# A two-layer hybrid block on one core: the root taken of the tanh, the input gate multiplied from PSUM, weight high parts on ScalarE in one stretch, key tiles read from PSUM

## The chip, the core and the metric

The kernel runs on one core of a Trainium2 chip. The metric is the device time of one execution in microseconds; lower is better. The kernel before took 1835.72 us as the median of 3 runs (1835.39 to 1839.09).

## The reference

Two layers act on 256 latent and 256 context tokens of width 1024. A layer normalises and modulates, runs four branches side by side (a state-space branch, grouped-query attention, differential attention and a gated linear recurrence), merges them with sigmoid gates, and ends in a convolutional feed-forward part. The last layer gives out the latent tokens alone. The change touches the recurrence and the keys of the grouped-query attention:

```python
def rglru_sequence(x_in, p, h0):                       # recurrence, 512 channels, both directions
    xr = dwconv(x_in, p['rg_conv_w'], p['rg_conv_b'], 1)
    for d in range(2):
        gate_a = blockdiag(xr, p['rg_wa'][d]) + p['rg_ba'][d]
        gate_x = blockdiag(xr, p['rg_wx'][d]) + p['rg_bx'][d]
        log_a = -8 * sigmoid(gate_a) * softplus(-p['rg_lambda'][d])
        a = exp(log_a)
        b = sqrt(-expm1(2 * log_a)) * (sigmoid(gate_x) * xr)
        h_sum += linear_scan(a, b, h0[d])              # context first, then latent
    return h_sum                                       # then times gelu(rgg)

kc = rmsnorm(heads(k_c), p['gqa_knorm_g'])             # keys of the context
kl = apply_rope(rmsnorm(heads(k_l), p['gqa_knorm_g']), cos, sin)
```

## The kernel before

Every matmul operand in fp32 is split into a high part, rounded to the fast matmul type, and a low part, the rest; a product is three matmuls (`mm3`, L267 to L269: low by high, high by low, high by high). `split` makes the parts: the high one by a cast, on ScalarE (L256, ACT in the profile) or on VectorE (L258, DVE), the low one by a subtraction (L251) on GpSimd (POOL) or DVE. For weights `whl` (L319) does so in tiles of 128x1024 named `whl`, four buffers of them. `turn` sets the engines by counting tiles: `turn[1]` is how often a low part goes to POOL, `turn[2]` how often a high part goes to DVE. In the stretch from the first recurrent pair to the end of the state-space branch `turn[1:] = 1, 2` holds: every low part on POOL, every second high part on DVE.

PSUM is two pools of four buffers each: `big` for projections, `small` for the rest. A `big` tile is free again when its last reader is done. The order of instructions on each engine is not written out: a scheduler with a timeline of its own chooses it when the program is built, so that a change in one function can move instructions elsewhere. On each engine instructions run in that order, and one that waits holds up those behind it.

In each layer, after the norm, the recurrent inputs are projected (`rg_in`), then come `rg_pair(0)`, `kvdt`, `rg_pair(1)`, `xbc(0)` and the state-space branch, beside which the recurrent branch is merged (`merge(3, ...)`).

`rg_pair` works on two channel tiles `c` by two directions `d`. Two small matmuls (L1021, L1024) give the gates; ACT takes tanh of both (L1022 to `t` in tile `B`, L1025 to `tx`), then exp (L1027, to `e`) and tanh (L1028, in `t`) of the decay. With `t` = tanh(u/2) and `e` = exp(-u), DVE forms 1 - a (L1030), minus (1 - a squared) (L1031) and a (L1032) on 128x1024; one ACT instruction takes the root for all of the pair (L1033, 128x2048, behind a load of its function table). DVE multiplies the gate (L1038), POOL the input (L1040, four of 128x512), then DVE scans (L1041, L1042, L1044), POOL adds the directions (L1054), DVE multiplies by the gelu (L1055) and the result is split into `bo` (ACT L256, DVE L251). The gelu of the second projection `rgg` stands between (L1048 to L1052).

`kvdt` (L652) projects key, step size and value columns for four token tiles into `big`, copies keys and steps to SBUF as `raw` (ACT L666, in a buffer called `xs`) and values (DVE L667), then works on all four together: squares (L671), sums (L673), the power on POOL (L676), rotary products (L608 to L619), scaling (L682), transposes on PE (L625) and the split into `kp`. `ssd_decay` follows with the softplus of the step sizes (L343 to L356).

Of the kernel before, what the change touches and what calls it, by code (L numbers as in the profile page):

```python
# [9 lines left out]
F32 = mybir.dt.float32  # L10
# [8 lines left out]
T = NL + NX  # L19
# [188 lines left out]
def _build(ctx, nc, tc, I, out, dbg):  # L208
# [19 lines left out]
    def big(n=T):  # L228
        p = pb.tile([128, 512], F32, name="big")
        return p[:, :n]  # L230
# [5 lines left out]
    def tt(name, n=512, dt=F32, bufs=None):  # L236

        x = tmp.tile([128, 512], dt, name=name, bufs=bufs or 3)
        return x[:, :n]
# [4 lines left out]
    def blk(ap, d):  # L244
        return ap.rearrange("p (h d) -> p h d", d=d)

    def bc(ap, shape):
        return ap.to_broadcast(shape)
# [287 lines left out]
    def tm(ps, w, t, h):  # L536

        kn = w[0].h.shape[1]
        for k in range(KT):
            mm3(ps, h[:, k, t * 128:(t + 1) * 128], w[k // kn][:, k % kn], k == 0, k == KT - 1)  # L540
# [14 lines left out]
    class Mixer:  # L555
# [96 lines left out]
        def kvdt(self):  # L652

            l, p, h = self.l, self.p, self.h
            w = wrows(l, "kvdt0", 2) + wrows(l, "kvdt1", 2)
            kp = self.long([128, 2, 2, T], "kp", 1, F32R)
            kh, kl = kp[:, 0], kp[:, 1]
            self.gk = Mat(kh, kl)
            self.gv = self.long([128, 4, 128], "gv")
            self.dt = sp.tile([128, 4, 16], F32, name="dt", bufs=1)  # L660
            raw = self.long([128, 2, T], "xs", 2).rearrange("p a t -> p (a t)")[:, :576]
            raw = raw.rearrange("p (t c) -> p t c", t=4)
            for t in range(4):
                ps = big(272)
                tm(ps, w, t, h)
                S.copy(raw[:, t], ps[:, 0:144])  # L666
                V.tensor_copy(self.gv[:, t], ps[:, 144:272])  # L667
            V.tensor_tensor(self.dt, raw[:, :, 128:144], bc(p["dtb"][:, None, :], [128, 4, 16]), op=OP.add)
            k = raw[:, :, 0:128]
            sq = tt("sq", bufs=2)  # L670
            S.activation(blk(sq, 128), k, AF.Square)  # L671
            ss = sp.tile([128, 8], F32, name="ss")
            V.tensor_reduce(ss, blk(sq, 64), axis=AX.X, op=OP.add)  # L673
            V.tensor_scalar(ss, ss, 1.0 / 64, EPS, op0=OP.mult, op1=OP.add)
            r = sp.tile([128, 8], F32, name="r64")
            G.tensor_tensor(r, ss, mhalf[:, :8], op=OP.pow)  # L676
            for t in range(0, 4, 2):
                d = blk(tt("fo", 256), 64)
                for z in range(2):
                    self.rope_of(d[:, 2 * z:2 * z + 2], blk(k[:, t + z], 64), t + z, 1, 2)  # L680
                d2 = tt("fo")
                V.tensor_tensor(d2.rearrange("p (h z c) -> p h z c", h=4, z=2), bc(d[:, :, None, :], [128, 4, 2, 64]),  # L682
                                bc(r[:, 2 * t:2 * t + 4, None, None], [128, 4, 2, 64]), op=OP.mult)
                v = self.twice(d2)
                for z in range(2):
                    ts = slice((t + z) * 128, (t + z + 1) * 128)
                    self.keys(v[:, 2 * z:2 * z + 2], kh[:, :, ts], kl[:, :, ts])
# [320 lines left out]
        def rg_pair(self, i, bm, xrs, bws):  # L1008

            l, p, h, n = self.l, self.p, self.h, self.n  # L1010

            es = [self.long([128, 2, T], "st", 3) for _ in range(2)]
            ta = self.long([128, 4, T], "B8")
            ts = [ta[:, 2 * c:2 * c + 2] for c in range(2)]
            xs = [self.long([128, 2, T], "st", 3), self.long([128, 2, T], "A4")]
            for c in range(2):
                for d in range(2):
                    pc = d * 4 + 2 * i + c
                    t, e, tx = ts[c][:, d], es[c][:, d], xs[c][:, d]
                    ps = small()  # L1020
                    PE.matmul(ps, bws[c][:, d * 2], xrs[c], start=True, stop=True)  # L1021
                    S.activation(t, ps, AF.Tanh, scale=0.5, bias=p["rba"][:, pc:pc + 1])  # L1022
                    px = small()
                    PE.matmul(px, bws[c][:, d * 2 + 1], xrs[c], start=True, stop=True)  # L1024
                    S.activation(tx, px, AF.Tanh, scale=0.5, bias=p["rbx"][:, pc:pc + 1])  # L1025
                    c1, c2 = p["rgc"][:, pc:pc + 1], p["rgm"][:, pc:pc + 1]
                    S.activation(e, t, AF.Exp, scale=c2, bias=c2)  # L1027
                    S.activation(t, t, AF.Tanh, scale=c1, bias=c1)  # L1028
                e2 = es[c]
                V.scalar_tensor_tensor(e2, e2, 1.0, ts[c], op0=OP.add, op1=OP.mult)  # L1030
                V.scalar_tensor_tensor(ts[c], e2, -2.0, e2, op0=OP.add, op1=OP.mult)  # L1031
                V.tensor_scalar(e2, e2, -1.0, 1.0, op0=OP.mult, op1=OP.add)  # L1032
            S.activation(ta, ta, AF.Sqrt, scale=-0.25)  # L1033
            wg = wcols(l, f"rgg{i}")
            for c in range(2):
                cp = 2 * i + c
                t, e, tx = ts[c], es[c], xs[c]
                V.scalar_tensor_tensor(tx, tx, 1.0, t, op0=OP.add, op1=OP.mult)  # L1038
                for d in range(2):
                    G.tensor_tensor(tx[:, d], tx[:, d], xrs[c], op=OP.mult)  # L1040
                V.tensor_tensor_scan(t[:, 0, NL:T], e[:, 0, NL:T], tx[:, 0, NL:T], 0.0, op0=OP.mult, op1=OP.add)  # L1041
                V.tensor_tensor_scan(t[:, 0, 0:NL], e[:, 0, 0:NL], tx[:, 0, 0:NL], t[:, 0, T - 1:T], op0=OP.mult,  # L1042
                                     op1=OP.add)
                V.tensor_tensor_scan(t[:, 1, ::-1], e[:, 1, ::-1], tx[:, 1, ::-1], 0.0, op0=OP.mult, op1=OP.add)  # L1044
                ps = big(n)
                fm(ps, wg[c], h, n)
                u = tt("sq", n, bufs=2)
                S.activation(u, ps, AF.Square)  # L1048
                V.tensor_scalar(u, u, 0.044715, 1.0, op0=OP.mult, op1=OP.add)
                V.tensor_tensor(u, u, ps, op=OP.mult)  # L1050
                S.activation(u, u, AF.Tanh, scale=math.sqrt(2.0 / math.pi))
                V.scalar_tensor_tensor(u, u, 1.0, ps, op0=OP.add, op1=OP.mult)  # L1052
                f = t[:, 0, :n]
                G.tensor_tensor(f, f, t[:, 1, :n], op=OP.add)  # L1054
                V.scalar_tensor_tensor(f, f, 0.5, u, op0=OP.mult, op1=OP.mult)  # L1055
                split(bm[cp][:, :n], f, V)
# [178 lines left out]
    for l in range(DEPTH):  # L1235
# [14 lines left out]
        turn[1] = NEVER  # L1250
        b3 = mx.branch()
        rin = [mx.rg_in(0, "bcm", 1), mx.rg_in(1, "xs", 2)]
        turn[1:] = 1, 2
        mx.rg_pair(0, b3, *rin[0])
        late_params(l, p)
        mx.kvdt()
# [92 lines left out]
```

## Time and profile before

| what | value |
|---|---|
| median of the runs | 1835.72 us |
| profiled execution, its own time | 1833.32 us |
| its span | 1831.2 us |
| mean granted clock of TensorE, share of full speed | 0.963 |
| PE busy | 1715.3 us, 94% |
| DVE busy | 1298.7 us, 71% |
| ACT busy | 904.4 us, 49% |
| POOL busy | 889.1 us, 49% |

The span is what the profile shows of an execution; its own time has 2.1 us around that. PE is TensorE's matmuls, whose ends are modelled, so its share says how much of the span had a matmul under way. Layer 0's recurrence and keys lie at about 70 to 190 us of the span, layer 1's at about 1170 to 1290 us. Durations of neighbours on one engine overlap by up to a tenth of a us.

### The profile page before, as it was taken

Reading aid. Unit: us, or ns where it says so; the run is one execution under the profiler, and the core shown is the slowest. Engines: PE = TensorE matmul, PEld = TensorE weight load, DVE = VectorE, ACT = ScalarE, POOL = GpSimd, SP = SyncE. Lnnn points to the kernel's source line nnn. Section 1 sums busy time; section 2 is a strip of 40 time slices with the busy share of each in tenths; the row PEclk is TensorE's granted clock in tenths of the full one; section 3 lists DMA queues with packets and bytes.
Section 4 is the critical chain, followed back from the end, with each engine's and each line's share of the span. In section 5 each row is a group of like instructions: output and inputs, shape, how many; then the busy total and the mean of one; then the engine's idle time right before and its main releaser. Section 6 shows DMA issues by size and latency. Waiting matters only on the chain.

```text
span 1831.2 us, 27922 instructions
## 1 busy us (share of the span) xinstructions
PE 1715.3 (94%) x10734; PEld 1499.3 (82%) x10734; DVE 1298.7 (71%) x2259; ACT 904.4 (49%) x1651; POOL 889.1 (49%) x536
## 2 busy tenths in 40 slices
PE   7968999999989998999999999966989999989999
PEld 1856788878788787987888888855888899989998
DVE  6798667666868676898856475698867668567664
ACT  3525544545444554465544343535445455556554
POOL 4364656252435657566543242465574244534443
PEclk8988999999989999999999999978989999989999
DMA  7211433131313355535645443222233133445553
GB/s 290 85 69 46 145 104 122 70 104 47 104 58 111 112 184 207 185 119 172 219 172 181 147 147 111 69 83 97 93 117 137 47 116 113 164 141 196 181 182 130
DMA packets 52036, 237.10 MB, mean 129 GB/s; under 512 B 9664, under 2 KB 12608, under 8 KB 34496
## 3 DMA queue, kind: packets, MB, share of 16 engines
q1 hardware_dynamic: 28080, 179.46, 28.1%
q10 hardware_dynamic: 23824, 55.86, 9.6%
q8 instruction: 85, 1.39, 0.3%
q14 instruction: 47, 0.39, 0.1%
HBM read 234.18 MB, written 1.11 MB: 128 GB/s over the span
## 4 chain that ended last, share of the span: by engine, by line
PE 44%; DVE 9%; DMA 2%; POOL 2%; ACT 2%; issue 2%; DVEq 0%; ACTq 0%; POOLq 0%; SPq 0%
PE big L267 13%; PE big L268 13%; PE big L269 13%; DVE whl L251 1%; DMA w<-in_w 1%; DVE fo L435 1%; POOL whl L251 1%; DVE fo L552 1%; DMA wa<-in_w 1%; PE small L781 1%; PE small L589 1%; ACT whl L256 1%; DVE whl L258 0%; DVE B L1044 0%; PE small L1021 0%
## 5 line engine op out<-in xcount | busy, mean ns | idle before, releaser
L251 POOL TENSOR_TENSOR whl<-w,whl 128x1024 fp32r<-128x1024 f32 (+3 forms) x194 | 453.8, 2342 | 525.8 <-ACT whl L256 428.5
L267 PE MATMUL big<-hh,whl 128*128 128x256 f32 (+1 forms) x1632 | 549.9, 341 | 25.6 <-POOL whl L251 22.7
L268 PE MATMUL big<-hl,whl 128*128 128x256 f32 (+1 forms) x1632 | 550.9, 339 | 0.8 <-POOL hl L251 0.8
L269 PE MATMUL big<-hh,whl 128*128 128x256 f32 (+1 forms) x1632 | 550.9, 339 | 0.0
L256 ACT CAST whl<-w 128x1024 fp32r<-128x1024 f32 (+2 forms) x314 | 308.5, 987 | 169.1 <-PE big L269 83.4
L267 PEld LDWEIGHTS big<-hh,whl 128*128 128x128 f32 x1632 | 313.2, 194 | 60.3 <-POOL whl L251 23.8
L268 PEld LDWEIGHTS big<-hl,whl 128*128 128x128 f32 x1632 | 314.3, 193 | 33.7 <-issue 2.8
L269 PEld LDWEIGHTS big<-hh,whl 128*128 128x128 f32 x1632 | 314.2, 193 | 33.1 <-issue 3.6
L251 DVE TENSOR_TENSOR whl<-w,whl 128x1024 fp32r<-128x1024 f32 (+2 forms) x150 | 206.3, 1377 | 68.6 <-ACT whl L256 68.3
L552 DVE SCALAR_TENSOR_TENSOR fo<-big,pp,fo 128x510 f32<-128x510 f32 (+2 forms) x224 | 141.4, 634 | 72.1 <-ACT fo L544 68.5
L431 POOL TENSOR_TENSOR wa<-wa,crow 128x1024 f32<-128x1024 f32 x48 | 125.9, 2626 | 75.5 <-DVE fo L435 44.2
L268 PE MATMUL big<-whl,hh 128*128 128x256 f32 (+1 forms) x512 | 149.6, 293 | 1.9 <-POOL whl L251 1.9
L267 PE MATMUL big<-whl,hl 128*128 128x256 f32 (+1 forms) x512 | 148.3, 291 | 2.3 <-DVE sq L1052 1.4
L269 PE MATMUL big<-whl,hh 128*128 128x256 f32 (+1 forms) x512 | 149.6, 293 | 0.0
L269 PE MATMUL big<-act,whl 128*128 128x256 f32 (+1 forms) x392 | 125.6, 321 | 0.0
L268 PE MATMUL big<-act,whl 128*128 128x256 f32 (+1 forms) x392 | 125.4, 320 | 0.0
L267 PE MATMUL big<-act,whl 128*128 128x256 f32 (+1 forms) x392 | 125.3, 320 | 0.0
L544 ACT ACTIVATE fo<-big,pp 128x512 f32<-128x512 f32 (+1 forms) x104 | 71.1, 684 | 90.4 <-PE big L269 82.3
L267 PE MATMUL big<-bo,whl 128*128 128x512 f32 (+1 forms) x256 | 89.3, 353 | 20.8 <-ACT bo L256 13.3
L268 PEld LDWEIGHTS big<-whl,hh 128*128 128x128 f32 x512 | 100.2, 196 | 3.8 <-POOL whl L251 2.1
L267 PEld LDWEIGHTS big<-whl,hl 128*128 128x128 f32 x512 | 100.0, 196 | 3.8 <-DVE sq L1052 1.7
L269 PEld LDWEIGHTS big<-whl,hh 128*128 128x128 f32 x512 | 100.3, 196 | 2.2 <-issue 2.1
(302 smaller groups left out, 3359.7 us busy)
## 6 DMA issues: line engine op xcount, KB each, us to landing
w<-in_w SPq DMA_DIRECT2D x136, 1024.0 KB, 4.9
wa<-in_w ACTq DMA_DIRECT2D x64, 512.0 KB, 3.6
w<-in_w SPq DMA_DIRECT2D x16, 768.0 KB, 4.2
w<-in_w SPq DMA_DIRECT2D x16, 640.0 KB, 3.8
bcm<-in_w ACTq DMA_DIRECT2D x14, 512.0 KB, 3.6
q<-csd ACTq DMA_DIRECT2D x24, 256.0 KB, 4.3
wa<-in_w SPq DMA_DIRECT2D x11, 512.0 KB, 8.5
xm<-in_xT ACTq DMA_DIRECT2D x8, 512.0 KB, 7.0
```

The source lines that it names most:

```text
L251: eng.tensor_tensor(o, v, hi.bitcast(F32), op=OP.subtract)
L256: S.copy(m.h, v)
L267: PE.matmul(ps, a.l, b.h, start=start, stop=False)
L268: PE.matmul(ps, a.h, b.l, start=False, stop=False)
L269: PE.matmul(ps, a.h, b.h, start=False, stop=stop)
L431: G.tensor_tensor(w, w, cr, op=OP.mult)
L435: V.scalar_tensor_tensor(scr, w, 1.0, cr, op0=OP.mult, op1=OP.mult, accum_out=o)
L544: S.activation(o, ps, AF.Identity, scale=wt[:, nc_ + c:nc_ + c + 1], bias=b[:, c:c + 1])
L552: V.scalar_tensor_tensor(os_, is_, wt[:, j * nc_ + c:j * nc_ + c + 1], os_, op0=OP.mult, op1=OP.add)
L589: PE.transpose(ps[:, i * 128:(i + 1) * 128], s, ident)
L781: PE.matmul(ops[t][hs, pr * 128:(pr + 1) * 128], self.gv[:, k0 + kb, hs], ets[z][:, kb * 128:(kb + 1) * 128], start=kb == 0, stop=kb == kn ...
```

## The change

Four edits. First, in `rg_pair` the three DVE products ahead of the root go: the root is taken of 0.25 tanh(u/2), and afterwards DVE multiplies by 1 + e, which gives the same half of sqrt(1 - a squared); a is `e` itself. Second, the input gate's tanh stays in PSUM (ACT writes `px` in place), DVE multiplies (px + 1) by the input straight from there (L1022 of after), and the product with the root is on DVE in place of POOL (L1032 of after). Third, `turn[2]` is NEVER in the stretch, so ACT makes the high parts of all its weights. Fourth, `kvdt` has no copy `raw`: squares, steps, values and rotary products read the projection's PSUM tile, two token tiles at a time, and values are copied by ACT.

```diff
@@ kvdt
-            raw = self.long([128, 2, T], "xs", 2).rearrange("p a t -> p (a t)")[:, :576]
-            raw = raw.rearrange("p (t c) -> p t c", t=4)
-            for t in range(4):
-                ps = big(272)
-                tm(ps, w, t, h)
-                S.copy(raw[:, t], ps[:, 0:144])
-                V.tensor_copy(self.gv[:, t], ps[:, 144:272])
-            V.tensor_tensor(self.dt, raw[:, :, 128:144], bc(p["dtb"][:, None, :], [128, 4, 16]), op=OP.add)
-            k = raw[:, :, 0:128]
-            sq = tt("sq", bufs=2)
-            S.activation(blk(sq, 128), k, AF.Square)
...
             for t in range(0, 4, 2):
                 d = blk(tt("fo", 256), 64)
+                sq = tt("sq", 256, bufs=2)
                 for z in range(2):
-                    self.rope_of(d[:, 2 * z:2 * z + 2], blk(k[:, t + z], 64), t + z, 1, 2)
+                    ps = big(272)
+                    tm(ps, w, t + z, h)
+                    with tc.high_priority():
+                        S.activation(sq[:, z * 128:z * 128 + 128], ps[:, 0:128], AF.Square)
+                        S.copy(self.gv[:, t + z], ps[:, 144:272])
+                        V.tensor_tensor(self.dt[:, t + z], ps[:, 128:144], p["dtb"], op=OP.add)
+                        self.rope_of(d[:, 2 * z:2 * z + 2], blk(ps[:, 0:128], 64), t + z, 1, 2)
+                ss = sp.tile([128, 8], F32, name="ss")[:, :4]
+                V.tensor_reduce(ss, blk(sq, 64), axis=AX.X, op=OP.add)
...
+                G.tensor_tensor(r, ss, mhalf[:, :4], op=OP.pow)
@@ rg_pair
-                    S.activation(tx, px, AF.Tanh, scale=0.5, bias=p["rbx"][:, pc:pc + 1])
+                    S.activation(px, px, AF.Tanh, scale=0.5, bias=p["rbx"][:, pc:pc + 1])
+                    V.scalar_tensor_tensor(tx, px, 1.0, xrs[c], op0=OP.add, op1=OP.mult)
...
-                e2 = es[c]
-                V.scalar_tensor_tensor(e2, e2, 1.0, ts[c], op0=OP.add, op1=OP.mult)
-                V.scalar_tensor_tensor(ts[c], e2, -2.0, e2, op0=OP.add, op1=OP.mult)
-                V.tensor_scalar(e2, e2, -1.0, 1.0, op0=OP.mult, op1=OP.add)
-            S.activation(ta, ta, AF.Sqrt, scale=-0.25)
+            S.activation(ta, ta, AF.Sqrt, scale=0.25)
...
-                V.scalar_tensor_tensor(tx, tx, 1.0, t, op0=OP.add, op1=OP.mult)
-                for d in range(2):
-                    G.tensor_tensor(tx[:, d], tx[:, d], xrs[c], op=OP.mult)
+                V.scalar_tensor_tensor(t, e, 1.0, t, op0=OP.add, op1=OP.mult)
+                V.tensor_tensor(tx, tx, t, op=OP.mult)
@@ main loop
-        turn[1:] = 1, 2
+        turn[1:] = 1, NEVER
```

The scheduler's order moves with it. On POOL, layer 0, first recurrent pair: ahead of the pieces below stand the low parts of the four `kvdt` weight tiles, and the first `whl` of 128x1024 is that of the second pair's `rgg`. Before:

```order
L251 TENSOR_TENSOR whl<-w,whl 128x544 x4
L1040 TENSOR_TENSOR st<-st,bcm 128x512 x2
L1040 TENSOR_TENSOR A_729<-A_729,bcm 128x512 x2
L598 TENSOR_TENSOR tab_3977<-cst,rp 128x2x64
L601 TENSOR_TENSOR tab_3977<-cst,rp 128x2x32 x2
L1054 TENSOR_TENSOR B_727<-B_727 128x512 x2
L251 TENSOR_TENSOR whl<-w,whl 128x1024 x4
```

And now, on the same engine at the same place (L1046 is before's L1054):

```order
L251 TENSOR_TENSOR whl<-w,whl 128x544 x4
L1046 TENSOR_TENSOR B_727<-B_727 128x512 x2
L251 TENSOR_TENSOR whl<-w,whl 128x1024
L598 TENSOR_TENSOR tab_3976<-cst,rp 128x2x64
L601 TENSOR_TENSOR tab_3976<-cst,rp 128x2x32 x2
L676 TENSOR_TENSOR r_958<-ss,mhalf 128x4
L251 TENSOR_TENSOR whl<-w,whl 128x1024 x3
```

The four input products are gone, the rotary table (`tab`) stands behind the first low part, and both additions of the directions stay ahead of that part.

On DVE, the same place, from the root to the last scan (`st` and `A` are the gated inputs, `B` the decay's tile, `sq` the gelu). Before:

```order
L1038 SCALAR_TENSOR_TENSOR st<-st,B_727 128x1024
L1038 SCALAR_TENSOR_TENSOR A_729<-A_729,B_727 128x1024
L1052 SCALAR_TENSOR_TENSOR sq<-sq,big 128x512
L1041 SCALAR_TENSOR_TENSOR B_727<-st 128x256
L667 COPY gv<-big 128x128
L611 TENSOR_TENSOR fo<-xs,tab_1007 128x128
L617 TENSOR_TENSOR fth<-xs,tab_1007 128x128
L1042 SCALAR_TENSOR_TENSOR B_727<-st,B_727 128x256
L667 COPY gv<-big 128x128
L611 TENSOR_TENSOR fo<-xs,tab_1007 128x128
L617 TENSOR_TENSOR fth<-xs,tab_1007 128x128
L1044 SCALAR_TENSOR_TENSOR B_727<-st 128x512
```

Now, from the last scan on (L1034 is before's L1042, L1047 its L1055; the rows ahead of these are two L1031, two L1032, the gelu and the other five scans):

```order
L1034 SCALAR_TENSOR_TENSOR B_727<-st,B_727,A_729 128x256
L1047 SCALAR_TENSOR_TENSOR B_727<-B_727,sq 128x512 x2
L673 TENSOR_REDUCE ss<-sq 128x4
L670 TENSOR_TENSOR dt<-big,rp 128x16
L611 TENSOR_TENSOR fo<-big,tab_915 128x128
L617 TENSOR_TENSOR fth<-big,tab_915 128x128
L670 TENSOR_TENSOR dt<-big,rp 128x16
L611 TENSOR_TENSOR fo<-big,tab_915 128x128
L617 TENSOR_TENSOR fth<-big,tab_915 128x128
L674 TENSOR_SCALAR ss<-ss 128x4
```

The readers of the key tiles stand behind all six scans and both products with the gelu, and they read `big`, the PSUM tile, where they read `xs` before.

On PE, in the softmax of layer 0's second half of grouped-query attention (L735 and L736, L731 and L732 of after, are the scores, L589 transposes, L781, L777 of after, the values). Before:

```order
L781 MATMUL small<-et,gv 64x128
L735 MATMUL small<-kp,q 128x512
L736 MATMUL small<-kp,q 128x512
L781 MATMUL small<-et,gv 64x128 x6
L268 MATMUL big<-whl,hh 128x256
L269 MATMUL big<-whl,hh 128x256
L267 MATMUL big<-whl,hl 128x256
```

Now, four softmax steps and the head of a fifth:

```order
L589 MATMUL small<-cst,e 128x128 x4
L777 MATMUL small<-et,gv 64x128
L731 MATMUL small<-kp,q 128x512
L732 MATMUL small<-kp,q 128x512
L589 MATMUL small<-cst,e 128x128 x4
L731 MATMUL small<-kp,q 128x512
L732 MATMUL small<-kp,q 128x512
L777 MATMUL small<-et,gv 64x128 x8
L589 MATMUL small<-cst,e 128x128 x4
L731 MATMUL small<-kp,q 128x512
L732 MATMUL small<-kp,q 128x512
L589 MATMUL small<-cst,e 128x128 x4
```

The projections that stood between the steps (L267 to L269) have moved to other places in this half; five steps stand in a row.

## Rows read from the trace of the kernel before

**Rows 1.** The page's first part: busy time, share of the span, instructions.

```profile
PE 1715.3 (94%) x10734; PEld 1499.3 (82%) x10734; DVE 1298.7 (71%) x2259; ACT 904.4 (49%) x1651; POOL 889.1 (49%) x536
```

**Rows 2.** Waits of PE, 90 to 190 us: us in total, times, longest.

```profile
PE big L267 <- POOL whl L251: 11.1, 1, 11.1
PE small L865 <- DVE cs L853: 4.0, 1, 4.0
PE small L625 <- DVE fo L682: 3.7, 1, 3.7
```

**Rows 3.** Waits of PE, 1190 to 1290 us.

```profile
PE big L267 <- ACT bo L256: 13.3, 1, 13.3
PE big L267 <- POOL whl L251: 9.2, 3, 6.3
PE small L625 <- DVE fo L682: 6.0, 2, 3.7
```

**Rows 4.** Timeline of ACT, 87 to 94 us: start, us, instruction, idle before.

```profile
87.09 0.63 ACT L1051 ACTIVATE sq<-sq 128x512 f32<-128x512 f32 x1
...
90.76 1.28 ACT L1033 ACT_TABLE_LOAD   x1 [0.28 <-DVE B L1031]
92.05 1.92 ACT L1033 ACTIVATE B<-B 128x2048 f32<-128x2048 f32 x1
```

**Rows 5.** Timeline of DVE, 107 to 132 us.

```profile
107.74 0.72 DVE L1042 TENSOR_TENSOR_SCAN B<-st,B,A 128x256 f32<-128x256 f32 x1
...
113.37 0.28 DVE L667 COPY gv<-big 128x128 f32<-128x128 f32 x1
...
131.17 0.68 DVE L682 TENSOR_TENSOR fo<-fo,r 128x512 f32<-128x512 f32 x1
```

**Rows 6.** Timeline of POOL, 108 to 121 us.

```profile
108.53 1.62 POOL L1054 TENSOR_TENSOR B<-B 128x512 f32<-128x512 f32 x1 [1.80 <-DVE B L1042]
110.12 10.69 POOL L251 TENSOR_TENSOR whl<-w,whl 128x1024 fp32r<-128x1024 f32 x4
```

**Rows 7.** Durations by line, whole span: ns min/median/max, first and last start.

```profile
L1030 DVE SCALAR_TENSOR_TENSOR st<-st,B x8: 1207/1226/3255, 78.6 to 1257.1; 128x1024 f32<-128x1024 f32 x8
L1041 DVE TENSOR_TENSOR_SCAN B<-st x4: 678/1756/2880, 97.5 to 1271.9; 128x256 f32<-128x256 f32 x4
L617 DVE TENSOR_TENSOR fth<-big,tab x24: 406/415/422, 296.8 to 1522.8; 128x256 f32<-128x256 f32 x24
L617 DVE TENSOR_TENSOR fth<-xs,tab x4: 278/1360/1383, 100.5 to 1200.0; 128x128 f32<-128x128 f32 x4
L258 DVE CAST whl<-w x30: 428/691/2790, 43.8 to 1334.7; 128x1024 fp32r<-128x1024 f32 x26, 128x544 fp32r<-128x544 f32 x4
```

**Rows 8.** Timeline of PE around the wait that ends at 112.96 us.

```profile
112.96 0.79 PE L267 MATMUL big<-hh,whl 128*128 128x512 f32 x1 [11.12 <-POOL whl L251]
113.55 0.63 PE L268 MATMUL big<-hl,whl 128*128 128x512 f32 x1
...
118.72 0.39 PE L269 MATMUL big<-hh,whl 128*128 128x512 f32 x1
```

**Rows 9.** Timeline of ACT, layer 0's second pair.

```profile
157.07 1.28 ACT L1033 ACT_TABLE_LOAD   x1 [4.49 <-DVE B L1031]
```

**Rows 10.** Timeline of ACT, 1252 to 1265 us, layer 1's second pair.

```profile
1252.96 1.04 ACT L256 CAST whl<-w 128x1024 fp32r<-128x1024 f32 x1
1253.89 0.82 ACT L1028 ACTIVATE B<-B,rgc 128x512 f32<-128x512 f32 x1
...
1261.72 1.28 ACT L1033 ACT_TABLE_LOAD   x1 [0.48 <-DVE B L1031]
1263.01 1.91 ACT L1033 ACTIVATE B<-B 128x2048 f32<-128x2048 f32 x1
```

**Rows 11.** Timeline of DVE, 1281 to 1283 us, the last scan there.

```profile
1281.09 1.19 DVE L1044 TENSOR_TENSOR_SCAN B<-st,A 128x512 f32<-128x512 f32 x1
```

**Rows 12.** Timeline of PE, 512 us, a softmax step of layer 0.

```profile
512.22 0.58 PE L735 MATMUL small<-B,q 128*128 128x256 f32 x1 [3.46 <-ACT e L741]
```

More of the change, by code (lines that the diff above doesn't have):

```diff
@@ L669, in kvdt @@
-            k = raw[:, :, 0:128]
-            sq = tt("sq", bufs=2)
-            S.activation(blk(sq, 128), k, AF.Square)
[L672 to L676, printed above, removed]
             for t in range(0, 4, 2):
                 d = blk(tt("fo", 256), 64)
+                sq = tt("sq", 256, bufs=2)
@@ L681, in kvdt @@
+                ss = sp.tile([128, 8], F32, name="ss")[:, :4]
+                V.tensor_reduce(ss, blk(sq, 64), axis=AX.X, op=OP.add)
+                V.tensor_scalar(ss, ss, 1.0 / 64, EPS, op0=OP.mult, op1=OP.add)
+                r = sp.tile([128, 8], F32, name="r64")[:, :4]
+                G.tensor_tensor(r, ss, mhalf[:, :4], op=OP.pow)
                 d2 = tt("fo")
                 V.tensor_tensor(d2.rearrange("p (h z c) -> p h z c", h=4, z=2), bc(d[:, :, None, :], [128, 4, 2, 64]),
-                                bc(r[:, 2 * t:2 * t + 4, None, None], [128, 4, 2, 64]), op=OP.mult)
+                                bc(r[:, :, None, None], [128, 4, 2, 64]), op=OP.mult)
```

## The prediction

> **What bounds the kernel now.** I read the page's first part, then the waits of PE by stretch, then the timelines of the engine that each wait names. PE has a matmul under way for 94% of the span and no other engine is above 71% [rows 1], so the kernel gains only where PE stands still or runs slowly. The two stretches that the change touches hold a good part of what PE loses: in layer 0 waits of 11.1, 4.0 and 3.7 us [rows 2], in layer 1 13.3, 9.2 and 6.0 us [rows 3], 47.3 us in all. Only two kinds of engine are named there, POOL's low parts of weights and something that DVE makes. The timelines say that both are one chain. In layer 0 the root starts on ACT at 92.05 us [rows 4]; from its end (93.97) DVE takes until 108.46 for the last scan [rows 5]; POOL adds the directions (start 108.53) and only then turns to the low part that PE needs, at 110.12 [rows 6]; PE goes on at 112.96 [rows 8]. In that queue the low part stands behind the recurrence, though it has nothing to do with it.
>
> A wait costs more than its length. After it the matmuls of 512 columns take 0.63 us in the record, and at 118.72 they take 0.39 [rows 8]: half of the clock's two levels (1.2 of 2.4 GHz) is granted for some 5 us, worth about 2.4 us of work.
>
> DVE is slower there than its instructions need. A scan of 256 columns takes 0.68 us at best and 2.88 at worst, L1030 1.23 in the middle and 3.26 at worst [rows 7], and the long ones lie where POOL is at work. POOL's four low parts together took 10.69 us, 2.7 each [rows 6], so I price one such meeting at 0 to 2.7 us and, where POOL works throughout, at 2.1 (2.88 less 0.68 and a little). Reading from PSUM makes a difference in the same line: L617 from `big` is 0.41 to 0.42 us in all 24 cases, from SBUF 0.28 to 1.38, at half the width [rows 7]. [...]
>
> **Part by part.** Everything is counted on the profiled execution, 1833.32 us (span 1831.2); the median of the runs is 2.4 us above it, and I add that at the end.
>
> *Work on DVE.* A pair loses two each of L1030, L1031, L1038 at 1.23 and of L1032, which I take at the 0.69 of a cast of that shape (L258), and gains four L1022 (128x512, one input in PSUM, nearest L682 with 0.68 [rows 5]), two L1031 and two L1032 of 128x1024, which I take at L1030's 1.23. That is 8.7 against 7.6 us: nearly nothing. What matters is where they stand: the three products were ahead of the root, L1022 can be done beside the tanhs. 28 casts, nearly all of L258, go from 0.69 on DVE to 1.04 on ACT [rows 7, 10]. POOL loses 16 input products.
>
> *Layer 0, first wait (11.1).* The root now needs ACT's own tanh alone. The last ACT instruction ahead of it in the new order is the gelu's tanh, done at 87.72 in the old trace [rows 4]; with one more narrow cast (under 1.04, say 0.6), the table load (1.28) and the root (1.92) it ends at about 91.5, 2.5 us earlier. Then DVE: four products of 1.23, three gelu instructions of at most 0.68, four scans of 0.68 and two of 1.19 [rows 5, 7, 11] make 12.1, less 0.1 of overlap each 10.8, and one meeting with POOL's narrow low part, 0 to 2.7, say 1.2: last scan at 103.5. POOL's second addition to 105.1, the low part to 107.5. But PE also needs a free `big` tile. Four tiles are in use, all by keys, and the first comes free with its second rotary product, which stands on DVE behind both products with the gelu. The second of these meets the low part and ends at about 108; reduce, steps and two rotary products (0.4 each at most) end at 109.3. So PE goes on at 109.3 and not at 112.96: 3.7 us. Bounds: 0 (every scan meets POOL) and 6.
>
> *Layer 0, second wait (3.7).* In the old trace DVE took 17.8 us from the key copy at 113.37 to the scaling at 131.17 [rows 5], through gelu products and softplus, with POOL's low parts alongside. The new order does the first half of the keys early and reads them from PSUM; two casts (1.4) are gone: 16.4 from 109.3 is 125.7. PE went on at 131.9, right behind that scaling, after a wait of 3.7 [rows 2], so its own work since 112.96 was 15.2; from 109.3, with four transposes more, it is there at 125.3. The wait shrinks to 0.4: 3.3 us. Bounds 0 and 3.7.
>
> *Layer 0, third wait (4.0).* It is for `cs`, a copy that stands on DVE behind five scans. The table load of that root waited 4.49 us for DVE [rows 9]; that goes. But two products more stand ahead of the copy (2.4). I take 2.0; bounds 0 and 4.0.
>
> *Layer 1, first waits (9.2 and 6.0).* The low part that PE waits for now stands ahead of POOL's additions, so it is no longer the last; the free `big` tile is, by the same reckoning about 1 us before the old end. The later, shorter wait for a low part (within the 9.2) goes. In their place comes a new one: the third projection after the keys needs the tile of the third key tile, whose rotary product stands behind most of the softplus; I put this wait at 6 us, as long as the 6.0 that it replaces. Net gain 4; bounds 0 and 8.
>
> *Layer 1, the long wait (13.3).* PE waits for `bo`, behind the last scan at 1282.28 [rows 11]. The root's table load began at 1261.72, though ACT's last recurrent instruction was done at 1254.71; ahead of that stood a cast (1.04) and a convolution's first step (0.7 by L682's width), which the new order puts behind the root [rows 10]. So the load can begin at 1253.0, and with the 4 us from above the root ends at 1252.2 instead of 1264.92. The new DVE order from there to the last scan: four products (4.9), six scans (5.1), six convolution pieces of at most 0.68 (3), five small ones (1.5), less overlap 13 us; POOL has up to four low parts there, 0 to 8.4 at 2.1 each. So the last scan ends at 1265.2 to 1273.6. The rows nearest to it, the scans of rows 7 with their 1.76 in the middle, say that most meet POOL; I take three meetings, 1271.5: 10.8 earlier, of which 4 are counted already. Gain here 6.8; bounds 3 and 13.
>
> *The casts.* 28 high parts on ACT cost 0.35 us more each, 9.8 if all were on the path. A low part on POOL takes 2.7 us [rows 6] and there are four buffers of such tiles, so most of that lies ahead of need; I charge 2, bounds -2 (DVE has 19 us less to do) and 9.8.
>
> Sum: -3.7 - 3.3 - 2.0 - 4 - 6.8 + 2 = -17.8, 1815.5 for an execution like the profiled one. From the median, 1835.72, that is 1817.9, say 1818.
>
> **The rivals.**
>
> *The gain stays in PSUM.* Key tiles are held from their last matmul until DVE has read them, behind scans and gelu products, where before ACT copied keys out. If each DVE instruction there meets POOL, PE waits for a `big` tile as long as it waited for the low part. For it: the order on DVE shown above. Against it: rotary products from PSUM met nobody in 24 cases [rows 7], and the last value copy came as late as 113.37 before, too [rows 5]. Then only the third wait, the long one and the casts count, -2 - 6.8 + 2, and about 1829. The Trainium skill, Perfetto Trace Analysis, section "Identifying Performance Opportunities", says that repeated bubbles can mean too little PSUM for the next tile; no row before shows PE waiting for such a tile for longer than a few us, and by this rule the time would be that of this rival.
>
> *The softmax that lost its cover: slower.* In layer 0's second half of grouped-query attention five softmax steps now stand on PE with no projection between them. A step whose scores wait for the exp on ACT cost 3.46 us in one row [rows 12]. Five make 17, and each such wait can be followed by up to 2.4 us at half clock [rows 8], 29 in all: 11 more than the gain, 1847. It decides from 3.6 us a step, a little above the one row there is. Against it: two steps are in flight at a time, and the fillers only moved within that half.
>
> *No change.* The recurrence ends earlier and PE meets the next thing that is late (DVE is busy for nearly all of these stretches), so the waits come back under other names: 0 to -3 us, 1834.
>
> **How the numbers follow.** A measurement of this kernel tells about 0.2% (3.7 us) from no change. Forecast 0.62, by itself 1806 to 1826; PSUM rival 0.18; no change 0.09; slower 0.11. Faster: all of the first, 0.16 of the second and 0.03 of the third, 0.81. Same: 0.02 of the second, 0.05 of the third and 0.02 of the last, 0.09. Slower 0.10. For the range the terms' bounds give 0 to 37 us of gain with the casts at 2; all at one end is unlikely, so low 1803. Above, 1832 takes in the PSUM rival and leaves out the slower one and half of no change.
>
> **What would show it.** Right: the root's table load follows a tanh with no wait for DVE; POOL has no 128x512 product with `bcm` or `xs`; PE's first wait in layer 0 ends 3 to 4 us earlier, released by DVE's reader of a `big` tile; the 13.3 is at most 6. Wrong: table loads that still wait for DVE, PE waits for `big` tiles of 8 us and more, waits for ACT's `whl` casts beside the state-space branch, or waits of the scores for ACT of over 3 us a step in layer 0's attention.

## The result, and the profile after

The changed kernel runs at 1808.68 us (median of 4 runs, 1806.92 to 1810.63) against 1836.38 for the kernel before beside it (4 runs, 1835.39 to 1839.09): ratio 0.9847, interval 0.983 to 0.9864, so 27.7 us faster. A second set of 4 gave 0.9839 (0.9825 to 0.9852). The profiled execution has a span of 1806.7 us, 24.5 less than before.

The first part of the page of after, against [rows 1]:

```profile
PE 1702.3 (94%) x10734; PEld 1490.2 (82%) x10734; DVE 1243.0 (69%) x2233; ACT 925.0 (51%) x1685; POOL 855.6 (47%) x522
```

With the same 10734 matmuls PE is busy for 13.0 us less, and it stands still for 11.5 us less (1831.2 - 1715.3 = 115.9 before, 104.4 now; 101.2 in the trace of the second set). The forecast counted waits only.

PE's waits, after, 90 to 190 us, against [rows 2]:

```profile
PE small L625 <- DVE fo L678: 5.6, 2, 5.0
PE big L267 <- DVE sq L1044: 3.0, 1, 3.0
PE small L861 <- DVE cs L849: 1.7, 1, 1.7
PE small L589 <- DVE gm L863: 1.2, 1, 1.2
PE big L267 <- DVE fth L617: 1.0, 1, 1.0
```

And 1182 to 1282 us, where layer 1 now lies, against [rows 3]:

```profile
PE big L267 <- ACT sq L668: 9.1, 1, 9.1
PE big L267 <- DVE dec L858: 5.3, 1, 5.3
PE big L267 <- DVE et L354: 4.0, 1, 4.0
```

The 11.1 behind POOL and the 13.3 for `bo` are gone. Three others have come in layer 1: for a key square on ACT, for something DVE makes at L858, and for the softplus (L354). In layer 0 a wait of 3.0 us is new too, for a `big` tile that the last gelu product (L1044) has yet to read.

After, ACT before the root of layer 0, against [rows 4]; then layer 1's second pair, against [rows 10]:

```profile
86.44 0.62 ACT L1043 ACTIVATE sq<-sq 128x512 f32<-128x512 f32 x1
87.08 1.28 ACT L1026 ACT_TABLE_LOAD   x1
88.38 1.92 ACT L1026 ACTIVATE B<-B 128x2048 f32<-128x2048 f32 x1
...
1238.04 0.66 ACT L1021 ACTIVATE small<-small,pp 128x512 f32<-128x512 f32 x1 [0.29 <-PE small L1020]
1238.72 1.28 ACT L1026 ACT_TABLE_LOAD   x1
```

Both table loads follow a tanh at once. DVE in layer 0, after, from the root's end to the scaling that PE waits for, against [rows 5], and POOL beside it, against [rows 6]:

```profile
90.33 3.53 DVE L1031 SCALAR_TENSOR_TENSOR B<-st,B 128x1024 f32<-128x1024 f32 x2 [2.49 <-ACT B L1026]
...
101.62 1.39 DVE L1034 TENSOR_TENSOR_SCAN B<-st,B,A 128x256 f32<-128x256 f32 x1
...
108.17 0.28 DVE L617 TENSOR_TENSOR fth<-big,tab 128x128 f32<-128x128 f32 x1
...
124.77 2.32 DVE L353 TENSOR_TENSOR et<-et 128x64 f32<-128x64 f32 x1
127.01 2.84 DVE L678 TENSOR_TENSOR fo<-fo,r 128x512 f32<-128x512 f32 x1
```

```profile
104.70 2.38 POOL L251 TENSOR_TENSOR whl<-w,whl 128x1024 fp32r<-128x1024 f32 x1
...
124.67 4.64 POOL L251 TENSOR_TENSOR whl<-w,whl 128x1024 fp32r<-128x1024 f32 x2 [4.07 <-ACT whl L256]
```

The last scan ends at 103.0 instead of 108.46. But while POOL makes two low parts, two instructions of DVE take 5.2 us that take 0.9 elsewhere (0.21 and 0.68 at the median or best of their lines): PE's second wait did not shrink, it grew from 3.7 to 5.0.

**Where the 24.5 us lie.** Start of the n-th of the 10734 matmul records, us: first column before, then each kernel less before, worked out from the traces (the other columns are the experiments below). Up to 750 is layer 0's recurrence and keys, 1500 to 3250 its attention, 6000 to 7250 layer 1's recurrence, keys and state-space part; locally the order of matmuls differs.

```
    n   before   after  root  keys casts root+keys root+casts keys+casts
  750    196.3    -8.0  -4.6  -7.1  -3.2   -7.7       -8.0       -2.4
 1500    324.5    -8.2  -4.8  -7.1  -3.3   -8.0       -8.1       -2.5
 3250    614.9   -11.4  -4.2  -5.1  -7.1   -7.4      -12.0       -5.2
 6000   1162.9    -8.0  -2.9  -3.0  -6.1   -6.0      -10.7       -3.2
 7250   1391.5   -24.5 -20.4   0.9 -16.6  -25.9      -30.8      -16.3
10733   1827.1   -24.5 -17.6   1.9 -16.7  -24.9      -29.4      -17.4
```

So 8 us come from layer 0's recurrence and keys, a net 0 from what lies between (3 gained in the attention and lost again behind it), and 16.5 from layer 1. Each column is a single execution, up to 3 us off the median of its kernel (root 3.1 and keys 2.2 above it, casts 2.7 below). A second trace of after has -7.8, -7.9, -11.3, -9.6, -27.2 and -26.8 at these six places: from 6000 on, a difference of under 3 us says little.

### The profile page after: what moved, and what is told of

Its sections match the earlier page's. It is cut to its first block, busy times and chain, and to the rows that moved or that the text cites. A ratio compares the mean times of both kernels' runs of the same rounds, so it can differ in the third digit from the quotient of the medians.

```text
span 1806.7 us, 27888 instructions
## 1 busy us (share of the span) xinstructions
PE 1702.3 (94%) x10734; PEld 1490.2 (82%) x10734; DVE 1243.0 (69%) x2233; ACT 925.0 (51%) x1685; POOL 855.6 (47%) x522
## 4 chain that ended last, share of the span: by engine, by line
PE 39%; DVE 5%; DMA 2%; POOL 2%; ACT 2%; issue 1%; ACTq 0%; POOLq 0%; DVEq 0%; SPq 0%
PE big L267 12%; PE big L268 12%; PE big L269 12%; DMA w<-in_w 1%; POOL whl L251 1%; DMA wa<-in_w 1%; POOL wa L431 1%; PE small L777 1%; ACT whl L256 1%; PE small L589 1%; DVE whl L251 1%; PE small L625 0%; DVE fo L552 0%; PE small L731 0%; DVE B L1033 0%
## 5 line engine op out<-in xcount | busy, mean ns | idle before, releaser
L267 PE MATMUL big<-hh,whl 128*128 128x256 f32 (+1 forms) x1632 | 549.0, 341 | 24.6 <-ACT sq L668 9.1
L269 PE MATMUL big<-hh,whl 128*128 128x256 f32 (+1 forms) x1632 | 549.6, 338 | 0.0
L256 ACT CAST whl<-w 128x1024 fp32r<-128x1024 f32 (+3 forms) x342 | 334.6, 985 | 171.3 <-PE big L269 81.9
L267 PEld LDWEIGHTS big<-hh,whl 128*128 128x128 f32 x1632 | 312.2, 193 | 61.0 <-issue 15.7
L269 PEld LDWEIGHTS big<-hh,whl 128*128 128x128 f32 x1632 | 314.4, 193 | 33.2 <-issue 3.4
L251 DVE TENSOR_TENSOR whl<-w,whl 128x1024 fp32r<-128x1024 f32 (+2 forms) x150 | 198.7, 1326 | 68.1 <-ACT whl L256 67.7
L267 PE MATMUL big<-whl,hl 128*128 128x256 f32 (+1 forms) x512 | 148.9, 292 | 3.5 <-DVE sq L1044 3.0
L269 PE MATMUL big<-whl,hh 128*128 128x256 f32 (+1 forms) x512 | 149.4, 292 | 0.0
L267 PE MATMUL big<-act,whl 128*128 128x256 f32 (+1 forms) x392 | 125.4, 320 | 4.1 <-POOL whl L251 4.1
L269 PE MATMUL big<-act,whl 128*128 128x256 f32 (+1 forms) x392 | 125.6, 321 | 0.0
L267 PEld LDWEIGHTS big<-whl,hl 128*128 128x128 f32 x512 | 100.1, 196 | 5.3 <-DVE sq L1044 3.2
L269 PEld LDWEIGHTS big<-whl,hh 128*128 128x128 f32 x512 | 100.4, 196 | 1.2 <-issue 1.0
L267 PE MATMUL big<-bo,whl 128*128 128x512 f32 (+1 forms) x256 | 89.1, 349 | 9.7 <-POOL whl L251 9.3
```

The costliest lines, as they stand in the source:

```text
L251: eng.tensor_tensor(o, v, hi.bitcast(F32), op=OP.subtract)
L256: S.copy(m.h, v)
L267: PE.matmul(ps, a.l, b.h, start=start, stop=False)
L269: PE.matmul(ps, a.h, b.h, start=False, stop=stop)
```

## Experiments

Three edits make up the change: the recurrent pair (root), the key tiles (keys), the high parts (casts). Every kernel was timed in 5 rounds beside the kernel before; ratios are to that.

**The recurrent pair alone** (the part of the diff in `rg_pair`).

> The kernel before with the recurrent pair alone changed (root of tanh, input gate read from PSUM, no product on POOL); key tiles and high parts as before. Theory A (the path theory, by the terms of the prediction): the root's table load no longer waits for DVE (0 instead of 0.5 to 4.5 us of wait), so the first wait of layer 0 falls by about 2.5 to 4, the third by about 2 and layer 1's 13.3 to about 6: 10 to 14 us faster. Rival B (the gain is DVE's relief by the 28 casts): this kernel gains at most 3 us. Theory C (the clock doubles it): the span falls by about twice the fall of PE's idle time, so that PE's busy time at an equal count of matmuls falls by 4 us or more; A without C has PE's busy time unchanged within 2 us.

Measured: 1812.32 us, ratio 0.9879 (0.9861 to 0.9897): 23 us, twice theory A's number, and far from B's 3. The root's table load waits for nobody, the wait for `bo` is gone in layer 1 altogether, and the waits there (1182 to 1282 us) are

```profile
PE big L267 <- POOL whl L251: 7.7, 3, 4.0
PE small L625 <- DVE fo L682: 5.6, 2, 4.4
PE small L589 <- ACT etot L859: 3.4, 1, 3.4
```

Theory C, as it was put, fails here: PE stands still 15.6 us less (1813.6 - 1713.3 = 100.3), its busy time falls by 2.0 only. By these totals an earlier root removes waits alone. What the clock gave all the same is worked out in the next section.

**The key tiles alone** (the part in `kvdt`).

> The kernel before with the key tiles alone taken from PSUM (squares, values and time steps read there, two tiles at a time); recurrence and high parts as before. Theory A: the recurrence still ends as late as before and the low part that PE waits for stands behind it, so layer 0's 11.1 and layer 1's 13.3 stay within 1.5 us; only the second wait (3.7) can go: 0 to 4 us faster. Rival (PSUM holds PE up): PE waits for big tiles through the whole recurrence, 4 us or more slower. Rival B (relief of DVE is what counts): the two casts and the SBUF reads saved give 3 to 6 us.

Measured: 1832.88 us, ratio 0.9985 (0.9974 to 0.9995), within A's bounds, but not by A's way. PE's waits in both layers, 60 to 190 and 1140 to 1300 us:

```profile
PE big L267 <- DVE fth L617: 13.3, 1, 13.3
...
PE big L267 <- ACT sq L668: 17.3, 1, 17.3
PE big L267 <- ACT bo L256: 6.4, 1, 6.4
```

The 11.1 did not stay as it was: it became 13.3 for a `big` tile. Both kernels reach that wait with the same 464 matmuls done, and this one goes on 2.0 us later. What it gains in layer 0 (7.1 us at matmul 750) lies behind it: the waits for the scaled keys (3.7) and for `cs` (4.0) are gone, and PE's busy time up to there falls by 4.9. Over half of that is lost again by matmul 6000, and layer 1 takes the rest with a 17.3. The rival that PSUM holds PE up is right about the wait and wrong about the time as a whole.

**The casts alone.**

```
-        turn[1:] = 1, 2
+        turn[1:] = 1, NEVER
```

> The kernel before with the high parts of the weights on ACT alone changed (28 casts leave DVE, each 0.35 us longer on ACT). Theory A: ACT is queued behind the chain of the recurrence too, and its casts stand ahead of the root: 2 us slower, bounds 2 faster and 10 slower. Rival B (DVE is the queue that everything waits for, and it is 19 us lighter here): 5 to 12 us faster, most of it in layer 1's 13.3.

Measured: 1818.92 us, ratio 0.9911 (0.9895 to 0.9926): 16.4 faster, where theory A had 2 slower. Rival B had the sign, though not the size. That DVE's casts hold others up could be seen in the kernel before, in the view of the line that makes low parts, on POOL (what its engine waited for: us, times):

```profile
  ACT whl L256: 428.5, 108
  DVE whl L258: 47.0, 17
```

A high part on DVE stands in the queue of the recurrence, and 17 low parts stood still for 47.0 us behind such casts. In this kernel that row is gone, but POOL then waits as long for ACT's casts alone (470.9 us, before 475.5 for both), so shorter waits of POOL are not where the gain comes from. DVE is busy for 24.5 us less (1274.2), and layer 1's last scan ends at 1272.1 instead of 1282.28, 10 us earlier, of which 6.1 were gained before that layer. Of PE's waits the one for POOL in layer 0 became 8.9 (before 11.1) and the one for `bo` in layer 1 5.8 (before 13.3), while layer 1's for POOL and for the scaled keys grew to 12.4 and 9.3. DVE's shorter queue is thus the likelier cause; no run here tells it apart from the earlier low parts that single matmuls wait for.

**The input product back on POOL** (after, with the product behind the root).

```
-  S.activation(px, px, AF.Tanh, ...);  V.scalar_tensor_tensor(tx, px, 1.0, xrs[c], ...)
+  S.activation(tx, px, AF.Tanh, ...)
...
-  V.tensor_tensor(tx, tx, t, op=OP.mult)
+  V.scalar_tensor_tensor(tx, tx, 1.0, t, op0=OP.add, op1=OP.mult)
+  for d in range(2): G.tensor_tensor(tx[:, d], tx[:, d], xrs[c], op=OP.mult)
```

> The kernel after, but the input gate's tanh goes to SBUF again, and the gate is applied behind the root by one product on DVE and two 128x512 products on POOL per column tile, as before; the root of tanh stays. Tells the two halves of the recurrence's edit apart. Theory A (what counts is that the root needs no DVE product ahead of it): 0 to 4 us slower than after, since POOL's products of about 1.1 us lie between root and scans. Rival D (what counts is that POOL's products and their meetings with DVE are gone): 8 us or more slower than after.

Measured: 1811.58 us, ratio 0.9866 (0.9848 to 0.9884), 3 to 5 us above the two medians of after, and its interval overlaps theirs. POOL's products took 1.3 to 2.3 us each in all but one case, more than the 1.1 of the expectation. Of the recurrence's edit the root of tanh is the larger part; D's 8 us are not reached.

**The casts in layer 1 only.**

```
-        turn[1:] = 1, 2
+        turn[1:] = 1, NEVER if l else 2
```

> The kernel before with the high parts on ACT alone changed, and only in layer 1 (14 of the 28 casts leave DVE; layer 0 keeps every second one on DVE). The kernel with all 28 on ACT was 16.4 us faster. Theory B1 (each cast that leaves DVE helps where it stood, because POOL's low part and PE wait for it behind DVE's recurrence): layer 0 as before, so that its 3 us in the recurrence and 4 to 5 us in the softmax half of grouped-query attention are missing, layer 1 keeps its 8 to 10: 8 to 10 us faster than before. Rival B2 (the gain is an accident of the order in which the scheduler now puts PE's work): the gain doesn't split by layer, 0 to 5 or 12 and more.

Measured: 1825.04 us, ratio 0.9938 (0.9925 to 0.995), 11.1 faster. By its trace it is 1.0 us behind the kernel before at matmul 3250 and gains 9.3 us between 6000 and the end. So B1 is the nearer, though the median gain is above its 8 to 10: each layer's casts help in that layer. Layer 0's are also what moved the order in the softmax half, which takes 1.7 to 3.9 us less between matmuls 1500 and 3250 in all nine traces with layer 0's casts on ACT (casts -3.8, root and casts -3.9, keys and casts -2.7, after -3.2) and not less without (root +0.6, root and keys +0.6, keys +2.0, this kernel +0.4).

**Two edits at a time: root and keys, root and casts, keys and casts.**

> The kernel after without the change of the casts (every second high part stays on DVE). If the casts' 16 us stand beside the recurrence's 23: 1824 to 1826, that is 16 slower than after. If both shorten the same chain (DVE's queue between the root and PE's next weight): 1808 to 1814, 0 to 5 slower than after.

> The kernel after without the change of the key tiles. Alone the key tiles gave 2.5 us. If that stands beside the rest: 1811. If the key tiles from PSUM hold PE up (the wait of 9.1 us for a key square in layer 1 and the 5.0 for the scaled keys in layer 0 are their doing): 1800 to 1807, faster than after. If without them the copies of keys on ACT and the SBUF reads on DVE come back onto the path: 1813 to 1818.

> The kernel after without the change of the recurrence: products ahead of the root and input product on POOL as before. If the recurrence is worth its 23 us on top of the others: 1830. If it shares most of them with the casts: 1812 to 1820, 4 to 11 slower than after. PE's idle time tells: with the root late, layer 1 keeps a wait of 6 us or more for bo behind the last scan.

Measured, medians in us, with the gain on the kernel before timed beside it:

```
root            1812.32  23.1      root + keys     1810.66  25.5
keys            1832.88   2.5      root + casts    1803.59  32.6
casts           1818.92  16.5      keys + casts    1817.13  19.0
                                   all (after)     1808.68  27.7
```

The single gains add up to 42; all together give 27.7, in the second set 30.7. On top of the other two the root is therefore worth 9 to 12 us, the casts 2 to 5, and the keys nothing or less: root and casts have a ratio of 0.983 (0.9809 to 0.9851), 2 to 5 us ahead of after, though the intervals overlap. Root and keys without the casts, 1810.66, is what the expectation gave if root and casts shorten the same queue, DVE between the root and PE's next weight. The kernel with keys and casts has 2.6 us left of the wait for `bo`, not the 6 that I expected: the casts alone had brought it from 13.3 to 5.8, the keys alone to 6.4.

**The key squares in PSUM** (after, to test what the 9.1 is), with after once more beside it.

```
-                sq = tt("sq", 256, bufs=2)
-                    ps = big(272)
-                        S.activation(sq[:, z * 128:z * 128 + 128], ps[:, 0:128], AF.Square)
-                V.tensor_reduce(ss, blk(sq, 64), axis=AX.X, op=OP.add)
+                    pt = big(400);  ps = pt[:, 0:272]
+                        S.activation(pt[:, 272:400], ps[:, 0:128], AF.Square)
+                        V.tensor_reduce(ss[:, 2*z:2*z+2], blk(pt[:, 272:400], 64), axis=AX.X, op=OP.add)
```

> The kernel after once more, for a comparison beside the three that follow: 1807 to 1811.

> The kernel after, but the key squares are written beside the key tile in its own PSUM bank and summed from there, so that they need no tile that the gelu's products still hold. Theory E (the trace's own words: PE's 9.1 us in layer 1 are the square on ACT that waits for its tile): the wait falls by 3 us or more, 3 to 6 us faster than after. Rival F (DVE's queue: the rotary products that free the same PSUM tile stand behind the scans and the last gelu product anyway): the wait is put down to the rotary product instead and stays within 1.5 us, 0 to 1.5 us faster.

Measured: after 1806.93 us, this 1801.29, ratio 0.9805 (0.9792 to 0.9819) against 0.9839 (0.9825 to 0.9852): 5.6 us faster than after, and the intervals don't meet. In after, the square that PE waits for stood on ACT until the last gelu product had freed its tile in SBUF (ACT, then DVE):

```profile
1197.68 0.45 ACT L668 ACTIVATE sq<-big 128x128 f32<-128x128 f32 x2 [5.82 <-DVE B L1047]
```

```profile
1195.10 2.55 DVE L1047 SCALAR_TENSOR_TENSOR B<-B,sq 128x256 f32<-128x256 f32 x1 [0.55 <-POOL B L1046]
```

With the square in PSUM the rotary products stand on DVE ahead of the last scans, and PE waits 4.4 instead of 9.1 (DVE, then PE, 1182 to 1282 us):

```profile
1189.35 0.28 DVE L617 TENSOR_TENSOR fth<-big,tab 128x128 f32<-128x128 f32 x1
1189.55 0.73 DVE L1034 TENSOR_TENSOR_SCAN B<-st,B 128x256 f32<-128x256 f32 x1
1190.21 2.78 DVE L1034 TENSOR_TENSOR_SCAN B<-st,B,A 128x256 f32<-128x256 f32 x1
```

```profile
PE big L267 <- DVE fth L617: 4.4, 1, 4.4
```

E, then: F named the next waiter rightly, but not that it would come earlier. Layer 0 gains as well: there the waits for the scaled keys fell from 5.6 to 3.7, and its trace is 3.6 us ahead of after's at matmul 750, so layer 1's wait alone is not the whole 5.6.

**The keys' scaling on ACT**, in after and in the kernel with root and casts.

```
-                V.tensor_tensor(d2..., bc(d...), bc(r...), op=OP.mult)
+                for j in range(4):
+                    S.activation(d2[:, j*128:(j+1)*128]..., bc(d[:, j]...), AF.Copy, scale=r[:, j:j+1])
```

> The kernel after, but the keys' scaling (two products of 128x512 with two inputs in SBUF in each layer, on DVE) is done by ACT in four pieces each. Theory G (layer 0's second wait stayed at 5.0 us because the scaling stands on DVE behind the softplus and takes 2.84 instead of 0.68 us where POOL's low parts run): the wait falls to under 1.5 us, and 3 to 7 us come off. Rival (the transposes then wait for the next thing on DVE, or the scheduler gives ACT's pieces a late place): 0 to 2 us.

> Recurrence and casts of after, key tiles as before, and the keys' scaling on ACT. The kernel without the last point ran at 1803.6 us and waits for the scaled keys for 3.7 us in layer 0 and 7.1 in layer 1. Theory G: those go, 4 to 10 us faster than that: 1794 to 1800. Rival: DVE's copies and softplus are next, 0 to 2 us.

Measured: in after 1801.74 us, ratio 0.9808 (0.9794 to 0.9822), 5.2 us faster; the 5.0 of layer 0 became 0.4, as G says, while the wait for `cs` rose to 5.7 and the first wait from 1.0 to 3.5. ACT's four pieces take 1.28 us here, while POOL makes a low part (123.91 to 126.28):

```profile
123.68 1.28 ACT L679 ACTIVATE fo<-fo,r 128x128 f32<-128x128 f32 x4
```

With root and casts 1801.64, ratio 0.9807 (0.9794 to 0.9821), against 0.983 (0.9809 to 0.9851) without it: 2.0 us faster by the medians, 3.4 by the gains on the kernel before, with intervals that overlap, so between the rival's number and G's. The waits for the scaled keys fell to 1.2 and 3.9 us rather than to nothing, and the one for `bo` rose from 5.8 to 8.8. The three fastest kernels (1801.3 to 1801.7) are not to be told apart; all three beat both before and after. Squares in PSUM and scaling on ACT together were not run.

## Why the prediction came out as it did

Direction and range held: 1808.7 lies in 1803 to 1832, 9.3 us below the forecast. The main cause held as well, the recurrence's chain that starts earlier; two terms did not, the casts and PE's busy time, and one that failed was made up by luck. Term by term:

- *Layer 0, first wait (-3.7).* Right, down to the working. Root's end 90.3 (forecast 91.5), last scan 103.0 (103.5), low part 107.1 (107.5); PE goes on at 108.59 (109.3), and what it waits for is the second rotary product from `big`, as said. Measured -4.4. A wait of 3.0 us for another `big` tile, which I did not foresee, stands ahead of it and cost nothing: PE reached the place 5.6 us later than before and had 1.0 left to wait there.
- *Second wait (-3.3).* The step that failed here was "it is there at 125.3" with DVE done at 125.7: I counted the softplus and the scaling at their short durations and gave no meeting with POOL to this place. They met POOL's two low parts, 4.3 us more, and the wait grew from 3.7 to 5.0. At matmul 600, behind it, the trace is 3.8 us ahead: what the first wait gave, and nothing from this term. The scaling on ACT shows it: the wait goes to 0.4, and that kernel is 9.8 us ahead at matmul 600.
- *Third wait (-2.0).* 4.0 became 1.7: right.
- I had -9.0 for these three, and the trace has -8.0 at matmul 750. That they are so near is partly luck: PE stands still only 5.6 us less up to there, and 2.5 are matmuls that took less time, which I had not counted.
- *Layer 1 (-4 and -6.8).* PE stands still 11.1 us less between matmuls 6000 and 7250, against -10.8. In parts: the first waits went from 15.2 to 13.1, not to 11.2: the new wait that I put at 6 is there with 4.0, behind the softplus, but of the 9.2, of which I left 5.2 for a free `big` tile, 9.1 are there under another name, the tile of the key squares. The long wait for `bo` is gone and 5.3 for something DVE makes at 1259.21 stands there, 1.2 less than the 6.5 that I left. The last scan came 12.9 us earlier, of the 20.9 by the clock of the trace, once the 8.0 gained before is taken off; I had 10.8.
- *What the sum left out: PE's busy time.* Between 6000 and 7250 PE's busy time falls by 5.4 us on top of the waits, over the whole span by 13.0. I had read that half clock follows a wait and priced it at 2.4 us each time [rows 8], for the slower rival, and did not put it on the gain side. The windows of before and after (us; busy times of PE, PEld, DVE, ACT, POOL; then PE's clock), the second of after where layer 1 now lies:

```profile
480.00:640.00 160.00, 147.66 (x853) 129.27 (x851) 120.51 (x212) 76.97 (x183) 82.60 (x52) 0.95 0.30 100
1190.00:1290.00 100.00, 68.26 (x369) 57.68 (x369) 86.03 (x121) 40.30 (x65) 60.31 (x33) 0.81 0.25 83
```

```profile
480.00:640.00 160.00, 148.79 (x871) 130.66 (x870) 115.99 (x205) 79.59 (x187) 84.44 (x54) 0.97 0.33 108
1182.00:1282.00 100.00, 78.35 (x440) 67.50 (x438) 72.53 (x121) 49.06 (x81) 53.16 (x32) 0.86 0.30 100
```

  In layer 1's recurrence (the second line) the granted clock rose from 0.81 to 0.86; in the softmax half (the first) from 0.95 to 0.97. The traces also tell how much of the 13.0 us this is. PE was busy for 96.8 us in stretches granted half clock before, and for 67.9 after. Matmuls of 512 columns start 0.43 us apart at it and 0.23 at full clock, behind the wait of [rows 8], so work takes about twice as long and half of that time is lost: 48.4 and 34.0 us, 14.5 less, against the 13.0 measured. With that half taken off, PE's busy time is 1666.9 us before and 1668.3 after, and between 1666.2 and 1670.3 in all 14 traces, while the busy times themselves run from 1699.5 to 1715.3. In layer 1's stretch the time at half clock fell from 28.9 to 18.7 us, which gives 5.1 of the 5.4. So the clock explains the shorter busy time but for a few us. The mean clock of a span hides this, as it also counts the half clock while PE stands still: the root alone has 0.973 over the span, near after's 0.975, but 86.1 us of work at half clock. Its 10.7 us less than before are worth 5.3; that its busy time fell by 2.0 only is the one difference of some size (3.3 us) that the clock leaves open.
- *The casts (+2).* The wrong sign. The cost on ACT is real (with the casts alone ACT is busy for 925.2 us instead of 904.4), but what counted was "DVE has 19 us less to do", which I put at -2 as a bound: alone they are worth 16.4, on top of the rest 2 to 5.
- *Softmax without its cover (the slower rival).* Five steps in a row do stand there, but the scores' waits for the exp, which I priced at 3.46 a step, fell from 6.8 us in four to 1.4 in two. Transposes wait for DVE instead (3.5 and 1.8). PE's waits, before, then after, 480 to 640 us:

```profile
PE small L735 <- ACT e L741: 6.8, 4, 3.5
```

```profile
PE small L589 <- DVE fth L826: 3.5, 1, 3.5
PE small L589 <- DVE ss L823: 1.8, 1, 1.8
PE small L731 <- ACT e L737: 1.4, 2, 0.8
```

  Between matmuls 1500 and 3250 PE stands still about as long as before (13.9 and 14.7 us), and the stretch is 3 us shorter because PE is busy for 4.0 less. The time at half clock, from 15.1 to 11.3 us, gives 1.9 of these; the two stretches do not hold quite the same matmuls.
- *PSUM holds the gain.* Half right: PE does wait for a `big` tile, 9.1 us in layer 1, and root and casts without the key tiles is at least as fast as the whole. The Trainium skill, Perfetto Trace Analysis, section "Identifying Performance Opportunities", says of a gap that repeats on the busy engine that it can mean too little SBUF or PSUM for the next tile. Here it is one long gap, but the run with the squares in PSUM agrees (9.1 to 4.4 us), and the tile that was short was one in SBUF.
- *Two slips in the working.* "Only two kinds of engine are named there" passes over the longest row, the 13.3 for `bo` from ACT [rows 3]; its term treats it rightly, as something behind the last scan. And the bounds with the casts charged at 2 give gains of 1 to 33 us, not 0 to 37; 33 is what the low end of 1803 stands for.

## What to carry to other kernels

Ask of each engine that works in order what stands behind the slow chain on it without belonging to it: here a weight's high part on DVE and its low part on POOL, both waiting for a recurrence. Ask also what stands in the chain's own queue: here weight casts among the scans. Price a moved instruction by the queue that it leaves as well as by the one that it joins. Gains of edits that shorten the same queue don't add, so measure each alone and each on top of the others: one of the three edits here, worth 2.5 us alone, gave nothing beside the other two. And count PE's work at half clock apart from its waits: of the 24.5 us here, 13.0 were busy time.

## What the runs showed of the hardware

How far POOL's low parts stretch an instruction of DVE depends on what it is and where its inputs lie. Four of the 16 products of L1022 (one input in PSUM) ran beside a low part for their whole length, as did one of the 4 sums of L673 nearly, and they took no longer than the rest. Products of two SBUF inputs and even tiny instructions of one took up to 2.2 us more (after, durations by line: ns min/median/max, first and last start):

```profile
L1022 DVE SCALAR_TENSOR_TENSOR st<-small,xs x4: 679/691/692, 135.2 to 1231.6; 128x512 f32<-128x512 f32 x4
L673 DVE TENSOR_REDUCE ss<-sq x4: 405/406/419, 107.6 to 1203.2; 128x4 f32<-128x256 f32 x4
L1032 DVE TENSOR_TENSOR A<-A,B x4: 1211/1980/3032, 95.2 to 1247.9; 128x1024 f32<-128x1024 f32 x4
L678 DVE TENSOR_TENSOR fo<-fo,r x4: 678/1763/2880, 112.0 to 1214.6; 128x512 f32<-128x512 f32 x4
L345 DVE TENSOR_SCALAR et<-dt x2: 180/1282/2383, 117.2 to 1204.6; 128x64 f32<-128x64 f32 x2
```

I had not expected the last: 128x64 with one input, 0.18 us alone and 2.38 beside a low part. The casts of the kernel before, one SBUF input each, do it too: 2.79 us at most where the median is 0.69 [rows 7]. The Trainium skill, SBUF — State Buffer, section "Who interferes with whom", has this: it names `cast` and `tensor_scalar` among the instructions that can take the shared ports, and `tensor_reduce` as one that never does. Both agree here, the second in the one sum that ran beside a low part (0.42 us). A low part of 128x1024 lasts 2.4 us, and a meeting cost up to about that whatever the size of what waits; it need not cost anything (L678 at 1211.55 took 0.69 us with a low part alongside throughout). A chain of many small instructions is what such an engine should not run beside.
